# Attention of a two-layer decoder trunk: three low parts move from GpSimd to VectorE, the value products lag the scores by three and five steps, and split and whole blocks alternate

## The chip, the cores and the metric

The kernel runs on one core of one Trainium2 chip. The metric is the time of one execution on the device in microseconds (us); lower is better. The core has five engines that run side by side: TensorE (PE; its weight loads are shown as PEld), VectorE (DVE), ScalarE (ACT), GpSimd (POOL) and SyncE (SP), which here only issues DMAs. Each works through its own instructions strictly in order. An instruction that has to wait for another engine therefore holds up everything behind it on its own engine.

## The reference, cut to what matters

The reference computes two decoder layers over 1024 positions with a model width of 1024. The change is in the first layer's attention: 12 heads, queries and keys of 96 features, values of 64, causal.

```python
def causal_dense_attention(q, k, v):          # q, k: 1024 x 12 x 96, v: 1024 x 12 x 64
    scale = dk ** -0.5
    sc = einsum('bqhd,bkhd->bhqk', q_blk, k) * scale
    sc = where(k_idx <= t_idx, sc, NEG)
    p = softmax(sc, axis=-1)
    return einsum('bhqk,bkhd->bqhd', p, v)

def reference(x, mem, positions, ...):
    for i in range(2):
        hn = rmsnorm(x, attn_norm_g[i])
        mix, q_cross = mla_mixer(...) if i % 2 == 0 else swa_mixer(...)   # MLA calls the attention above
        cross = memory_cross_attention(q_cross, mem_n, w_mem_kv[i])
        x = x + concatenate([mix, cross]) @ w_o[i]
        x = x + squared_relu_mlp(rmsnorm(x, mlp_norm_g[i]), mlp_w_up[i], mlp_w_down[i])
    return rmsnorm(x, final_norm_g)
```

All results must have float32 accuracy.

## The kernel before

**Split products.** The kernel's fast matmul form takes operands rounded to a shorter float (`fp32r` in the rows). To keep float32 accuracy a value is split: the high part is a rounded copy, made by ScalarE, and the low part (the rest) is the value minus the high part, made by a subtraction (`split`, L96 to L103). A product is then three matmuls: high by high, high by low, low by high. Whoever doesn't split uses the full float32 matmul, which counts as two instructions in the rows.

**The stages.** First the projections into queries, keys and values; then the attention of layer 0, the subject here; then the output projection (`pswo`), the MLP, and the same for layer 1. In the trace the attention runs from about 251 us to 516 us.

**The attention.** A head's scores are computed transposed: keys on the partitions, queries along the row. The 1024 queries are two groups G of 512, the 1024 keys are 8 blocks k of 128. Causality leaves 12 blocks (G, k) for each head; blocks on the diagonal are narrower: 512, 384, 256 or 128 queries wide (`width`). The table `blocks` sets their order within a head: (1,0), (0,0), (1,4), (0,1), (1,5), (0,2), (1,6), (0,3), (1,7), (1,1), (1,2), (1,3). I number these places 0 to 11. The last head has an order of its own, `blocks_end`.

For each block:

- `scores`: three matmuls of queries (`qh`, `ql`) and keys (`kh`, `kl`) into a bank of PSUM `pss`, with one more for the causal mask on the diagonal; then ScalarE's exponential into `p` (L855). A block in `WHOLE` is left so. Any other is split into `ph` (ScalarE) and `pl` (VectorE, L100).
- `values`: the product with the values, accumulated over a group's blocks in a PSUM bank `pso`. A whole block is one full float32 matmul with `vf`; a split block is three matmuls, `ph` by `vh`, `ph` by `vl`, `pl` by `vh`. When a group is done ScalarE copies it out (`on`) and DMAs store it. `vh` carries 64 columns of ones, which give the softmax denominators; `rc_split` and `rc_mul` later apply their reciprocals to the stored outputs (`psrc`).

The loop (from L956) walks the blocks of all heads in one sequence. At step n it issues the scores of block n, then some work of later heads, then the values of block n − 2 (`LV = 2`). Where one of the two blocks is 128 wide, their matmuls alternate.

The work of later heads is: `row_max`, a first cheap score product `psx` with VectorE's maximum over it (eight for each head, L729 to L731; those wider than 512 share one buffer of two banks); `max_row`, which transposes the maxima (`psxt`, L711) and writes them as a 97th feature into the queries by DMA; `head_tiles`, which loads the next-but-one head's queries and keys into single buffers `q32`, `k32` and splits them (high parts `qh`, `kh` by ScalarE, low parts `ql`, `kl` by GpSimd, `lo_eng`); and `v_tiles`, which splits the values (`vh` by ScalarE, `vl` by GpSimd, `vf` a copy by VectorE). The reciprocal tiles of `rc_split` use the buffers `q32` and `k32` too.

A scheduler then settles the order on each engine: it may move instructions ahead of where the code issues them when it thinks their inputs are ready.

Of the kernel before, what the change touches and what calls it, by code (L numbers as in the profile page):

```python
# [55 lines left out]
def trunk(  # L56
# [38 lines left out]

    def split(src, hi, lo, scale=None, lo_eng=None):  # L96

        if scale is None:
            nc.scalar.activation(hi, src, AF.Copy)  # L99
            (lo_eng or nc.vector).tensor_tensor(lo, src, f32(hi), ALU.subtract)  # L100
        else:
            nc.scalar.activation(hi, src, AF.Copy, scale=scale)
            nc.vector.scalar_tensor_tensor(lo, src, scale, f32(hi), ALU.mult, ALU.subtract)  # L103
# [588 lines left out]
    def head_tiles(h):  # L692
        r = slice((h % 2) * 64, (h % 2) * 64 + 64)
        q32 = hb.tile([96, S], F32, tag="q32", bufs=1, name=f"q32_{h}")
        k32 = hb.tile([96, S], F32, tag="k32", bufs=1, name=f"k32_{h}")
        nc.sync.dma_start(out=q32[0:64], in_=qn[h // 2][r, :])
        nc.sync.dma_start(out=q32[64:96], in_=qr[h // 4][(h % 4) * 32 : (h % 4) * 32 + 32, :])
        nc.sync.dma_start(out=k32[0:64], in_=kn[h // 2][r, :])
        nc.sync.dma_start(out=k32[64:96], in_=krs)
        qh, ql, kh, kl = bufs_[h % 3]  # L700
        if h in (1, 2):
            head_ones(h)
        split(q32, qh[0:96], ql[0:96], lo_eng=nc.gpsimd)
        split(k32, kh[0:96], kl[0:96], lo_eng=nc.gpsimd)

# [110 lines left out]
    def v_tiles(h):  # L816
        vh, vl, vf = vbufs[h % 2]
        src = v[:, :, h * 64 : (h + 1) * 64]
        if h < 2:
            nc.gpsimd.memset(f32(vh[:, :, 64:128]), 1.0)  # L820
            nc.gpsimd.memset(vf[:, :, 64:128], 1.0)
        nc.scalar.activation(vh[:, :, 0:64], src, AF.Copy)
        nc.gpsimd.tensor_tensor(vl, src, f32(vh[:, :, 0:64]), ALU.subtract)
        nc.vector.tensor_copy(vf[:, :, 0:64], src)

    blocks = [(1, 0), (0, 0), (1, 4), (0, 1), (1, 5), (0, 2), (1, 6), (0, 3), (1, 7), (1, 1), (1, 2), (1, 3)]

    blocks_end = [(1, k) for k in (0, 4, 5, 6, 7, 1, 2, 3)] + [(0, k) for k in range(4)]
    WHOLE = {(1, k) for k in (0, 4, 5, 6, 7)}
    probs, po_ = {}, {}  # L830
# [4 lines left out]
    def scores(h, G, k):  # L835
# [17 lines left out]
        def then():  # L853
            p = at.tile([P, 512], F32, tag="p", bufs=5, name=f"p{h}_{G}_{k}")
            nc.scalar.activation(p[:, c0:], ps, AF.Exp, scale=SC)  # L855
            if (G, k) in WHOLE or (h == H - 1 and G == 0):
# [9 lines left out]
    def values(h, G, k):  # L866

        vh, vl, vf = vbufs[h % 2]
        c0 = 512 - width(G, k)
        order = [b[1] for b in blocks if b[0] == G]  # L870
        first, last = k == order[0], k == order[-1]
        if first:
            po_[G] = ps1(f"pso{h}_{G}")
        po = po_[G]
        pr = probs.pop((h, G, k))
        mms = []
# [3 lines left out]

        if len(pr) == 1:
            mm(po[:, c0:], vf[:, k, :], pr[0][:, c0:], start=first, stop=last)
        else:
            ph, pl = pr
            mm(po[:, c0:], vh[:, k, :], ph[:, c0:], start=first, stop=False)
            mm(po[0:64, c0:], vl[:, k, :], ph[:, c0:], start=False, stop=False)
            mm(po[:, c0:], vh[:, k, :], pl[:, c0:], start=False, stop=last)

# [17 lines left out]
    def last_o(G, tmp):  # L906

        nc.vector.reciprocal(tmp, po_[G][64:128])
        nc.vector.tensor_tensor(qn[5][64:128, G * 512 : (G + 1) * 512], po_[G][0:64], tmp, ALU.mult)

# [44 lines left out]
    muls = iter(())  # L955
    for n in range(len(seq) + LV):  # L956
        ms, mv = [], []
        if n < len(seq):
            ms, then_s = scores(*seq[n])
        if n >= LV:  # L960
            mv, then_v = values(*seq[n - LV])

        mix = []
        if ms and mv and P in (width(*seq[n][1:]), width(*seq[n - LV][1:])):
            while ms and mv:
# [33 lines left out]
        if n == 10 * NB + LV + 1:  # L999
            rc_split(1)  # L1000
        if n == 10 * NB + LV + 8:
            muls = rc_mul(1)
        if n == 11 * NB + LV + 1:
            rc_split(2)
        if n == 11 * NB + LV + 6:
            muls = rc_mul(2)
    for _ in muls:
# [925 lines left out]
```

## Time and profile before

| | |
|---|---|
| median of 3 runs | 2217.64 us (2213.63 to 2220.11) |
| profiled execution | 2218.95 us, span 2216.1 us |
| mean granted TensorE clock | 0.986 |
| PE busy | 2151.1 us, 97% of the span |
| DVE / ACT / POOL busy | 1486.9 / 1018.5 / 235.1 us |

The span runs from the first to the last instruction; 2.85 us lie outside it. TensorE is busy nearly throughout, so the questions are where it is not, and where it is busy at a lower clock: the granted clock is a share of 2.4 GHz, and it is either 1.0 or 0.5 (1.2 GHz) at any moment, so a mean of 0.9 says that a fifth of the stretch ran at half speed. In a row of the timeline the first number is the start in us, the second the time taken; a bracket at the end gives how long the engine had been idle before and what ended that. Matmuls are pipelined: one starts before the one ahead has ended, so their pace is read from the starts.

### The profile page before, as it was taken

What the parts mean: (1) busy time and instruction counts of PE and PEld (TensorE: products, weight loads), DVE (VectorE), ACT (ScalarE), POOL (GpSimd) and SP (SyncE); (2) the same over time, 40 slices, a digit from 0 to 9 for tenths busy, and PEclk for the clock granted to TensorE, in tenths of its full rate; (3) what the DMA queues carried; (4) which work ended last, traced back from release to release, by engine and by line L of the source; (5) the groups of instructions that cost most, each with busy time, mean ns of one, the idle gap of its engine ahead of it and who ended that gap; (6) DMA issues with size and microseconds to landing.
All of it is one profiled execution on the core that took longest, in us unless ns stands there. A gap on an engine that the chain in (4) does not pass through costs nothing.

```text
span 2216.1 us, 28995 instructions
## 1 busy us (share of the span) xinstructions
PE 2151.1 (97%) x10005; PEld 1717.9 (78%) x10005; DVE 1486.9 (67%) x2789; ACT 1018.5 (46%) x2154; POOL 235.1 (11%) x263
## 2 busy tenths in 40 slices
PE   7999989999999999999999899999999999999998
PEld 6888656567878888888888788768788888788886
DVE  7566656566797777695757443675987776785565
ACT  5454455465543333344445363674633333444452
POOL 0023332220000000000001033350000000000000
PEclk9999989899999999999999999999999999999999
DMA  7202121134234444873534111113254445954442
GB/s 245 65 1 72 44 58 42 42 85 150 77 135 151 143 146 153 292 277 104 183 114 124 53 47 40 48 49 116 85 171 157 152 145 168 328 190 142 130 119 86
DMA packets 171232, 272.97 MB, mean 123 GB/s; under 512 B 15713, under 2 KB 71758, under 8 KB 171086
## 3 DMA queue, kind: packets, MB, share of 16 engines
q1 hardware_dynamic: 164228, 253.80, 35.6%
q0 software_dynamic: 4016, 13.12, 1.6%
q10 hardware_dynamic: 2842, 4.22, 0.6%
q8 instruction: 78, 1.28, 0.2%
q14 instruction: 68, 0.56, 0.1%
HBM read 181.69 MB, written 76.81 MB: 117 GB/s over the span
## 4 chain that ended last, share of the span: by engine, by line
PE 88%; DVE 5%; ACT 3%; DMA 1%; issue 1%; POOL 0%; SPq 0%; DVEq 0%; ACTq 0%; POOLq 0%
PE psu L1306 5%; PE psu L1307 5%; PE psu L1305 5%; PE psy L1591 5%; PE psy L1593 5%; PE psy L1592 5%; PE psz L1591 4%; PE psz L1593 4%; PE psz L1592 4%; PE psv L1305 4%; PE psv L1306 4%; PE psv L1307 4%; PE pss L845 4%; PE pso L879 3%; PE pswo L110 3%; PE pswo L108 3%
## 5 line engine op out<-in xcount | busy, mean ns | idle before, releaser
L855 ACT ACTIVATE p<-pss 128x512 f32<-128x512 f32 (+2 forms) x144 | 69.2, 487 | 96.6 <-PE pss L845 91.4
L99 ACT ACTIVATE i<-mr 128x512 fp32r<-128x512 f32 x78 | 49.3, 632 | 121.8 <-PE psu L1306 42.9
L731 DVE TENSOR_REDUCE m<-psx 128x1 f32<-128x640 f32 (+7 forms) x96 | 72.3, 754 | 43.9 <-PE psx L730 42.7
L1591 PE MATMUL psy<-g 128*128 128x512 f32 x256 | 99.9, 390 | 0.0
L1592 PE MATMUL psy<-g 128*128 128x512 f32 x256 | 99.6, 389 | 0.0
L1593 PE MATMUL psy<-g 128*128 128x512 f32 x256 | 99.4, 390 | 0.0
L100 DVE TENSOR_TENSOR pl<-p,ph 128x512 fp32r<-128x512 f32 (+3 forms) x80 | 73.1, 917 | 30.3 <-ACT ph L99 30.2
L99 ACT ACTIVATE g<-i 128x512 fp32r<-128x512 f32 x79 | 49.7, 629 | 93.2 <-PE psz L1592 46.2
L100 DVE TENSOR_TENSOR g<-i,g 128x512 fp32r<-128x512 f32 x79 | 55.3, 700 | 46.0 <-ACT g L99 45.8
L99 ACT ACTIVATE uh<-i 128x512 fp32r<-128x512 f32 x66 | 41.6, 631 | 86.2 <-PE psy L1592 40.7
L100 DVE TENSOR_TENSOR uh<-i,uh 128x512 fp32r<-128x512 f32 x66 | 45.5, 690 | 44.3 <-ACT uh L99 44.2
L1591 PE MATMUL psz<-g 128*128 128x512 f32 x192 | 74.7, 389 | 0.0
L1592 PE MATMUL psz<-g 128*128 128x512 f32 x192 | 74.7, 389 | 0.0
L1593 PE MATMUL psz<-g 128*128 128x512 f32 x192 | 74.7, 389 | 0.0
L100 DVE TENSOR_TENSOR i<-mr,i 128x512 fp32r<-128x512 f32 x78 | 53.7, 688 | 24.2 <-ACT i L99 24.2
L845 PE MATMUL pss<-qh,kh 97*128 97x512 f32 (+2 forms) x144 | 68.4, 478 | 0.6 <-DMA qh<-mhl 0.6
L1694 POOL TENSOR_TENSOR wsr<-wsr,gcol 128x1024 f32<-128x1024 f32 x12 | 24.2, 2017 | 355.3 <-DVE ul L1336 284.1
L1516 DVE TENSOR_TENSOR mqf<-mqq,mqf 128x512 f32<-128x512 f32 x64 | 43.1, 687 | 26.3 <-DMA mqq<-in_mlp_w_down_dram 26.0
L845 PE MATMUL pss<-ql,kh 97*128 97x512 f32 (+2 forms) x144 | 60.5, 420 | 0.0
L99 ACT ACTIVATE i<-d 128x512 fp32r<-128x512 f32 x44 | 27.8, 633 | 70.0 <-PE psu L1306 39.6
L1593 PEld LDWEIGHTS psy<-g 128*128 128x128 f32 x256 | 48.0, 188 | 10.0
L1592 PEld LDWEIGHTS psy<-g 128*128 128x128 f32 x256 | 48.1, 188 | 9.9
(623 smaller groups left out, 7018.8 us busy)
## 6 DMA issues: line engine op xcount, KB each, us to landing
i<-hd SPq DMA_DIRECT2D x154, 256.0 KB
hd<-uh SPq DMA_DIRECT2D x76, 256.0 KB
hd<-ul SPq DMA_DIRECT2D x76, 256.0 KB
mr<-in_mlp_w_up_dram SPq DMA_DIRECT2D x36, 512.0 KB
hd<-x SPq DMA_DIRECT2D x72, 256.0 KB
mr<-hd SPq DMA_DIRECT2D x70, 256.0 KB
d<-in_mlp_w_up_dram SPq DMA_DIRECT2D x32, 512.0 KB
mqq<-in_mlp_w_down_dram SPq DMA_DIRECT2D x32, 512.0 KB
```

The source lines that it names most:

```text
L99: nc.scalar.activation(hi, src, AF.Copy)
L100: (lo_eng or nc.vector).tensor_tensor(lo, src, f32(hi), ALU.subtract)
L108: nc.tensor.matmul(ps, ah, bh, start=first and i == 0, stop=False)
L731: nc.vector.reduce_max(m8s[h][:, i : i + 1], ps[:, :n], axis=AX, negate=True)
L845: return lambda: nc.tensor.matmul(o, a, b, skip_group_check=True, **kw)
L855: nc.scalar.activation(p[:, c0:], ps, AF.Exp, scale=SC)
L1305: nc.tensor.matmul(ps, wh[:, k, :], xh[:, k, :], start=p in (1, 2, 5) and k == 0, stop=False, skip_group_check=True)
L1306: nc.tensor.matmul(ps, wh[:, k, :], xl[:, k, :], start=False, stop=False, skip_group_check=True)
L1307: nc.tensor.matmul(ps, wl[:, k, :], xh[:, k, :], start=False, stop=k == 3, skip_group_check=True)
L1591: nc.tensor.matmul(ps, ah[:, j, :], bh, start=p in (1, 5, 2) and k == 0, stop=False, skip_group_check=True)
L1592: nc.tensor.matmul(ps, ah[:, j, :], bl, start=False, stop=False, skip_group_check=True)
L1593: nc.tensor.matmul(ps, al[:, j, :], bh, start=False, stop=k == NP - 1, skip_group_check=True)
```

## The change

There are three parts.

1. In `split` the choice of engine is dropped: `ql`, `kl` and `vl` are subtracted by VectorE, not GpSimd.
2. The values are issued in two parts. At step n come first the low part of block n − 5 (`LB = 5`: the one matmul with `pl`, only for split blocks), then the rest of block n − 3 (`LV = 3`: the whole block, or the two matmuls with `ph`). The buffers follow: `p` 5 to 4, `pl` 3 to 4. The start of `rc_split` and `rc_mul` is now 6 and 11 steps into the head behind each group of heads.
3. Block (1,2) is whole for each head, so that in `blocks` every second block is split; the last head's order becomes (1,0), (1,1), (1,4), (1,3), (1,5), (1,2), (1,6), (1,7), then the four of G = 0, with (1,1) and (1,3) split. Before it was (1,0), (1,4) to (1,7), then (1,1), (1,2), (1,3) split, then the four of G = 0.

```diff
-    def split(src, hi, lo, scale=None, lo_eng=None):
+    def split(src, hi, lo, scale=None):
         if scale is None:
             nc.scalar.activation(hi, src, AF.Copy)
-            (lo_eng or nc.vector).tensor_tensor(lo, src, f32(hi), ALU.subtract)
+            nc.vector.tensor_tensor(lo, src, f32(hi), ALU.subtract)
...
-        split(q32, qh[0:96], ql[0:96], lo_eng=nc.gpsimd)
-        split(k32, kh[0:96], kl[0:96], lo_eng=nc.gpsimd)
+        split(q32, qh[0:96], ql[0:96])
+        split(k32, kh[0:96], kl[0:96])
...
-        nc.gpsimd.tensor_tensor(vl, src, f32(vh[:, :, 0:64]), ALU.subtract)
+        nc.vector.tensor_tensor(vl, src, f32(vh[:, :, 0:64]), ALU.subtract)
...
-    WHOLE = {(1, k) for k in (0, 4, 5, 6, 7)}
+    def whole(h, G, k):
+        return k not in (1, 3) if G else h == H - 1
...
-            p = at.tile([P, 512], F32, tag="p", bufs=5, name=f"p{h}_{G}_{k}")
+            p = at.tile([P, 512], F32, tag="p", bufs=4, name=f"p{h}_{G}_{k}")
-            pl = at.tile([P, 512], F32R, tag="pl", bufs=3, name=f"pl{h}_{G}_{k}")
+            pl = at.tile([P, 512], F32R, tag="pl", bufs=4, name=f"pl{h}_{G}_{k}")
...
+        if late and whole(h, G, k):
+            return [], lambda: None
+        if late:
+            mm(po[:, c0:], vh[:, k, :], probs.pop((h, G, k, "late"))[:, c0:], start=False, stop=last)
...
-    LV = 2
+    LV, LB = 3, 5
...
+        for lag, late in ((LB, True), (LV, False)):
+            if 0 <= n - lag < len(seq):
+                a, b = values(*seq[n - lag], late)
+                mv += a
+                then.append(b)
...
-        if n == 6 * NB + LV + 3:
-            rc_split(0)
-        if n == 7 * NB + LV:
-            muls = rc_mul(0)
...
+            if n == GRP[c + 1] * NB + LB + 1:
+                rc_split(c)
+            if n == GRP[c + 1] * NB + LB + 6:
+                muls = rc_mul(c)
```

What this makes of TensorE's order is shown at the passage from the fourth head to the fifth (`_1_0` is the fifth head's first block; the names lack the head's number, the last number only counts). Before:

```order
L879 MATMUL pso_1_3131<-pl_1_1_3260,vh_2459 128x512
L845 MATMUL pss_1_0_3296<-qh_2445,kh_2447 128x512
L845 MATMUL pss_1_0_3296<-ql_2446,kh_2447 128x512
L845 MATMUL pss_1_0_3296<-qh_2445,kl_2448 128x512
L729 MATMUL psx_5_3302<-kh_2451,qh_2449 128x512
L729 MATMUL psx_5_3302<-kh_2451,qh_2449 128x256
L730 LDWEIGHTS identb
L730 MATMUL psx_5_3302<-dmask,identb 128x128
L879 MATMUL pso_1_3131<-ph_1_2_3274,vh_2459 128x512
L879 MATMUL pso_1_3131<-ph_1_2_3274,vl_2460 64x512
L879 MATMUL pso_1_3131<-pl_1_2_3275,vh_2459 128x512
```

The low part `pl_1_2` is used right behind its `ph_1_2`, with only one block of scores between two such low parts. In the changed kernel the same place reads:

```order
L852 MATMUL pss_1_0_3266<-ql_2446,kh_2447 128x512
L882 MATMUL pso_1_3130<-ph_1_1_3236,vh_2459 128x512
L852 MATMUL pss_1_0_3266<-qh_2445,kl_2448 128x512
L882 MATMUL pso_1_3130<-ph_1_1_3236,vl_2460 64x512
L729 MATMUL psx_5_3275<-kh_2451,qh_2449 128x512
L729 MATMUL psx_5_3275<-kh_2451,qh_2449 128x256
L730 LDWEIGHTS identb
L730 MATMUL psx_5_3275<-dmask,identb 128x128
L852 MATMUL pss_0_0_3284<-qh_2445,kh_2447 128x512
L882 MATMUL pso_1_3130<-p_1_2_3248,vf_2461 128x512
```

Here `ph_1_1` stands alone; its low part `pl_1_1` comes only after two more blocks of scores, (0,0) and (1,4), and two more `psx`; block (1,2) has become one product of the whole `p`.

VectorE's order at the same place, where `m` is the maximum over a `psx`. Before:

```order
L100 TENSOR_TENSOR pl_1_1_3260<-p_1_1_3257,ph_1_1_3259 128x512
L731 TENSOR_REDUCE m_5_3244<-psx_6_3278 128x1
L100 TENSOR_TENSOR pl_1_2_3275<-p_1_2_3272,ph_1_2_3274 128x512
L731 TENSOR_REDUCE m_5_3244<-psx_5_3302 128x1
L100 TENSOR_TENSOR pl_1_3_3290<-p_1_3_3287,ph_1_3_3289 128x512
L731 TENSOR_REDUCE m_5_3244<-psx_3_3321 128x1
L100 TENSOR_TENSOR pl_0_0_3318<-p_0_0_3315,ph_0_0_3317 128x512
L731 TENSOR_REDUCE m_5_3244<-psx_4_3340 128x1
```

In the changed kernel:

```order
L100 TENSOR_TENSOR pl_1_1_3237<-p_1_1_3234,ph_1_1_3236 128x512
L731 TENSOR_REDUCE m_5_3224<-psx_6_3250 128x1
L100 TENSOR_TENSOR kl_1881<-k_6_3313,kh_1880 96x1024
L731 TENSOR_REDUCE m_5_3224<-psx_5_3275 128x1
L100 TENSOR_TENSOR pl_1_3_3263<-p_1_3_3260,ph_1_3_3262 128x512
L824 COPY vf_2461<-v 128x8x64
L731 TENSOR_REDUCE m_5_3224<-psx_3_3296 128x1
L100 TENSOR_TENSOR ql_1879<-q_6_3312,qh_1878 96x1024
L100 TENSOR_TENSOR pl_0_0_3293<-p_0_0_3290,ph_0_0_3292 128x512
L731 TENSOR_REDUCE m_5_3224<-psx_4_3307 128x1
```

The subtraction `pl_1_2` is gone; `kl` and `ql` of the seventh head have come in, `kl` ahead of the maximum over `psx_5`, `ql` ahead of `pl_0_0`.

## Rows read from the trace of the kernel before

**Rows 1.** Page, part 1: busy us (share of the span) xinstructions of each engine

```profile
PE 2151.1 (97%) x10005; PEld 1717.9 (78%) x10005; DVE 1486.9 (67%) x2789; ACT 1018.5 (46%) x2154; POOL 235.1 (11%) x263
```

**Rows 2.** Busy time by stretch: stretch, length, five engines, clock, DMA; attention and parts

```profile
251.00:516.00 265.00, 244.75 (x1152) 160.78 (x1153) 164.61 (x216) 150.89 (x301) 70.21 (x39) 0.93 0.25 61
251.00:280.00 29.00, 22.76 (x111) 14.56 (x112) 23.96 (x24) 15.65 (x30) 16.19 (x10) 0.97 0.25 55
280.00:425.00 145.00, 134.00 (x638) 88.26 (x637) 87.07 (x115) 79.77 (x162) 36.03 (x20) 0.91 0.18 42
425.00:445.00 20.00, 17.85 (x71) 11.70 (x69) 9.32 (x14) 11.05 (x21) 5.94 (x3) 0.83 0.39 92
445.00:516.00 71.00, 70.13 (x340) 46.26 (x339) 44.26 (x63) 44.42 (x90) 12.06 (x6) 0.98 0.33 95
```

**Rows 3.** Waits from 251 to 516 us: who for whom, total, times, longest

```profile
PE pso L879 <- DVE pl L100: 16.2, 14, 2.0
PE psx L729 <- ACT kh L99: 2.1, 1, 2.1
PE psx L729 <- DVE m L731: 1.0, 2, 0.7
```

**Rows 4.** Timeline, 341 to 348 us: GpSimd, VectorE, TensorE

```profile
341.99 2.38 POOL L100 TENSOR_TENSOR kl<-k,kh 96x1024 fp32r<-96x1024 f32 x1 [10.86 <-ACT kh L99]
...
342.46 2.46 DVE L100 TENSOR_TENSOR pl<-p,ph 128x512 fp32r<-128x512 f32 x1 [0.38 <-ACT ph L99]
344.84 0.94 DVE L731 TENSOR_REDUCE m<-psx 128x1 f32<-128x768 f32 x1
...
344.97 0.50 PE L879 MATMUL pso<-pl,vh 128*128 128x512 f32 x1 [1.62 <-DVE pl L100]
347.91 0.80 PE L879 MATMUL pso<-pl,vh 128*128 128x512 f32 x1 [0.48 <-DVE pl L100]
```

**Rows 5.** Groups by line and shape: count, busy us, mean ns, idle before

```profile
L100 DVE TENSOR_TENSOR pl<-p,ph 128x512 fp32r<-128x512 f32 x47 | 53.6, 1143 | 25.9 <-ACT ph L99 25.7
...
L100 DVE TENSOR_TENSOR i<-mr,i 128x512 fp32r<-128x512 f32 x78 | 53.7, 688 | 24.2 <-ACT i L99 24.2
...
L100 DVE TENSOR_TENSOR wsl<-wsr,wsh 128x1024 fp32r<-128x1024 f32 x6 | 8.6, 1428 | 12.7 <-ACT wsh L99 12.7
L100 DVE TENSOR_TENSOR wf<-wsr,wf 128x1024 fp32r<-128x1024 f32 x6 | 7.3, 1224 | 15.6 <-ACT wf L99 15.6
...
L99 ACT ACTIVATE kh<-k 96x1024 fp32r<-96x1024 f32 x11 | 11.6, 1052 | 0.0
```

**Rows 6.** Timeline of TensorE, one head from `psxt` to `psxt`

```profile
359.39 0.28 PE L711 MATMUL psxt<-ident,m 128*8 128x128 f32 x1
...
368.28 0.50 PE L879 MATMUL pso<-pl,vh 128*128 128x512 f32 x1 [1.57 <-DVE pl L100]
371.24 0.50 PE L879 MATMUL pso<-pl,vh 128*128 128x512 f32 x1 [0.81 <-DVE pl L100]
380.17 0.27 PE L711 MATMUL psxt<-ident,m 128*8 128x128 f32 x1
```

**Rows 7.** Timeline of TensorE: a split block's three products, a whole block's pair

```profile
498.17 0.39 PE L879 MATMUL pso<-ph,vh 128*128 128x512 f32 x1
...
498.96 0.49 PE L938 MATMUL psrc<-rTq,sel 4*128 4x512 f32 x1
...
500.38 1.02 PE L879 MATMUL pso<-p,vf 128*128 128x512 f32 x2
501.33 0.49 PE L938 MATMUL psrc<-rTq,sel 4*128 4x512 f32 x1
```

**Rows 8.** Busy time by stretch, 5 us each, behind and with narrow blocks

```profile
420.00:425.00 5.00, 5.00 (x29) 3.21 (x28) 3.07 (x6) 1.18 (x3) 0.00 (x0) 1.00 0.02 5
425.00:430.00 5.00, 5.00 (x23) 3.62 (x22) 2.14 (x5) 2.27 (x7) 0.00 (x0) 0.85 0.32 75
...
490.00:495.00 5.00, 5.00 (x24) 3.10 (x22) 1.12 (x3) 3.98 (x9) 0.00 (x0) 1.00 0.12 28
```

More of the change, by code (lines that the diff above doesn't have):

```diff
@@ L822, in v_tiles, with blocks_of @@
         nc.scalar.activation(vh[:, :, 0:64], src, AF.Copy)
-        nc.gpsimd.tensor_tensor(vl, src, f32(vh[:, :, 0:64]), ALU.subtract)
+        nc.vector.tensor_tensor(vl, src, f32(vh[:, :, 0:64]), ALU.subtract)
         nc.vector.tensor_copy(vf[:, :, 0:64], src)
     blocks = [(1, 0), (0, 0), (1, 4), (0, 1), (1, 5), (0, 2), (1, 6), (0, 3), (1, 7), (1, 1), (1, 2), (1, 3)]
-    blocks_end = [(1, k) for k in (0, 4, 5, 6, 7, 1, 2, 3)] + [(0, k) for k in range(4)]
-    WHOLE = {(1, k) for k in (0, 4, 5, 6, 7)}
+    blocks_end = [(1, k) for k in (0, 1, 4, 3, 5, 2, 6, 7)] + [(0, k) for k in range(4)]
+    def blocks_of(h):
+        return blocks if h < H - 1 else blocks_end
+    def whole(h, G, k):
+        return k not in (1, 3) if G else h == H - 1
     probs, po_ = {}, {}
@@ L853, in then @@
         def then():
-            p = at.tile([P, 512], F32, tag="p", bufs=5, name=f"p{h}_{G}_{k}")
+            p = at.tile([P, 512], F32, tag="p", bufs=4, name=f"p{h}_{G}_{k}")
             nc.scalar.activation(p[:, c0:], ps, AF.Exp, scale=SC)
-            if (G, k) in WHOLE or (h == H - 1 and G == 0):
+            if whole(h, G, k):
                 probs[(h, G, k)] = (p,)
@@ L864, in scores, with values @@
         return mms, then
-    def values(h, G, k):
+    def values(h, G, k, late):
         vh, vl, vf = vbufs[h % 2]
         c0 = 512 - width(G, k)
-        order = [b[1] for b in blocks if b[0] == G]
+        order = [b[1] for b in blocks_of(h) if b[0] == G]
         first, last = k == order[0], k == order[-1]
[L872 to L875, printed above, removed]
         mms = []
@@ L879, in mm @@
             mms.append(lambda: nc.tensor.matmul(o, a, b, skip_group_check=True, **kw))
-        if len(pr) == 1:
-            mm(po[:, c0:], vf[:, k, :], pr[0][:, c0:], start=first, stop=last)
-        else:
[L884 to L887, printed above, removed]
+        if first and not late:
+            po_[(h, G)] = ps1(f"pso{h}_{G}")
+        po = po_[(h, G)]
+        if late and whole(h, G, k):
+            return [], lambda: None
+        if late:
+            mm(po[:, c0:], vh[:, k, :], probs.pop((h, G, k, "late"))[:, c0:], start=False, stop=last)
+        else:
+            pr = probs.pop((h, G, k))
+            if len(pr) == 1:
+                mm(po[:, c0:], vf[:, k, :], pr[0][:, c0:], start=first, stop=last)
+            else:
+                ph, probs[(h, G, k, "late")] = pr
+                mm(po[:, c0:], vh[:, k, :], ph[:, c0:], start=first, stop=False)
+                mm(po[0:64, c0:], vl[:, k, :], ph[:, c0:], start=False, stop=False)
+                last = False
         def then():
@@ L906, in last_o @@
     def last_o(G, tmp):
-        nc.vector.reciprocal(tmp, po_[G][64:128])
-        nc.vector.tensor_tensor(qn[5][64:128, G * 512 : (G + 1) * 512], po_[G][0:64], tmp, ALU.mult)
+        po = po_[(H - 1, G)]
+        nc.vector.reciprocal(tmp, po[64:128])
+        nc.vector.tensor_tensor(qn[5][64:128, G * 512 : (G + 1) * 512], po[0:64], tmp, ALU.mult)
     GRP = [0, 6, 10, 11]
@@ L946, in trunk @@
     head_tiles(1)
-    LV = 2
+    LV, LB = 3, 5
     NB = len(blocks)
-    seq = [(h,) + b for h in range(H) for b in (blocks if h < H - 1 else blocks_end)]
+    seq = [(h,) + b for h in range(H) for b in blocks_of(h)]
     ahead = {}
@@ L955, in trunk @@
     muls = iter(())
-    for n in range(len(seq) + LV):
-        ms, mv = [], []
+    for n in range(len(seq) + LB):
+        ms, mv, then = [], [], []
         if n < len(seq):
             ms, then_s = scores(*seq[n])
-        if n >= LV:
-            mv, then_v = values(*seq[n - LV])
+        for lag, late in ((LB, True), (LV, False)):
[3 more added lines that the diff above has]
+                then.append(b)
         mix = []
-        if ms and mv and P in (width(*seq[n][1:]), width(*seq[n - LV][1:])):
+        if ms and mv and P in [width(*seq[n - lag][1:]) for lag in (0, LV, LB)]:
             while ms and mv:
@@ L983, in trunk @@
             f()
-        if n >= LV:
-            then_v()
+        for f in then:
+            f()
         next(muls, None)
@@ L994, in trunk @@
             nc.scalar.activation(sel, sel32, AF.Copy)
-        if n == 6 * NB + LV + 3:
-            rc_split(0)
-        if n == 7 * NB + LV:
-            muls = rc_mul(0)
[L999 to L1006, printed above, removed]
+        for c in range(3):
+            if n == GRP[c + 1] * NB + LB + 1:
+                rc_split(c)
+            if n == GRP[c + 1] * NB + LB + 6:
+                muls = rc_mul(c)
     for _ in muls:
```

## The prediction

> **What bounds the kernel now.** I read the page's busy times first: TensorE is busy for 2151.1 of 2216.1 us [rows 1]. What can be gained lies in the remaining 65 us and in stretches at half clock. Next come the busy times by stretch. In the attention, 251 to 516 us, TensorE is busy for 244.75 of 265 us and its mean granted clock is 0.93 [rows 2]. So 20.25 us are idle. The clock has two levels, 1.2 and 2.4 GHz, and a mean of 0.93 means that 14% of the stretch ran at the lower one. What was done there would have taken half as long, so 0.07 × 265 = 18.6 us are lost to it (17.2 to 19.9 by the rounding of 0.93). The two add up to 38.9 us, and nothing else in the stage can be given back. The other engines are far from full there: VectorE 164.61 us, ScalarE 150.89, GpSimd 70.21.
>
> The waits name who ends TensorE's idle time: 16.2 of the 20.25 us end with VectorE's `pl`, in 14 waits; one of 2.1 us ends with ScalarE's `kh`, two of 1.0 us in all with the maxima `m` [rows 3]. The timeline shows why `pl` is late [rows 4]. A subtraction `pl` of 128x512 that begins at 342.46 takes 2.46 us. GpSimd's `kl` runs from 341.99 for 2.38 us, and `pl` ends about half a microsecond behind it; TensorE stood idle for 1.62 us until then. The groups say the same: these 47 `pl` take 1143 ns on average, while VectorE's subtraction of the same shape takes 688 ns elsewhere [rows 5]. So VectorE almost stands still while GpSimd subtracts, and TensorE uses `pl` too early to sit that out.
>
> **The change part by part.** *Engine.* GpSimd's subtractions leave; VectorE gets them. Their shapes on VectorE are not in the trace; the nearest rows are subtractions of 128x1024, 1224 ns, and 1428 ns for those that run beside GpSimd's multiplications [rows 5]. I take 1.22 us, since GpSimd now does next to nothing in this stage; 1.43 is the other end. The values' low part has the shape of the 688 ns row. In the stage 11 heads have their queries and keys split (the count of `kh` in [rows 5]), which adds 22 × 1.22 = 26.8 us to VectorE, and 12 their values, 12 × 0.69 = 8.3. It gives back as much, 8.3, for the `pl_1_2` of 12 heads, and 47 × (1.143 − 0.688) = 21.4 us of slowed `pl`: 164.6 + 26.8 + 8.3 − 8.3 − 21.4 = 170 us of some 238. VectorE stays under three quarters and can't bound the stage by its sum. It can by its order, and that is the wait that the change adds. `kl` waits for ScalarE's `kh`, which waits for the last scores that read the old keys; behind `kl` in VectorE's queue stands the maximum over `psx_5`, and TensorE's `psx_4` needs the buffer that this maximum frees. Between the two, TensorE has two blocks of 512 with the mask, a whole product and `psx_3`. By the pace of rows 7, three products in 0.79 us and a pair in 0.95, that is at least 2 × 0.8 + 0.95 = 2.5 us. VectorE needs 1.22 for `kl` and 0.94 [rows 4] for the maximum, 2.2 us in all. It fits with little to spare, and `kl` can begin earlier than I count, so I cost it at nothing. If the cover is gone it costs up to the whole of `kl`.
>
> *Lag.* `pl` is now used five blocks behind its scores. Three more blocks of 1 to 2 us each lie between, more than the longest `pl` wait of 2.0 us [rows 3], and the cause of the slow `pl` is gone too. So I let the 16.2 us go. `ph` and the whole `p` get one block more, which costs TensorE nothing; it has the same matmuls in another order.
>
> *Whole (1,2).* Three fast matmuls become one full one. From the first of the three to the next product (`psrc`) is 498.96 − 498.17 = 0.79 us, from the pair to the same kind of product 501.33 − 500.38 = 0.95 [rows 7]. That is 0.16 us more for each of 12 heads: 1.9 us lost. Other neighbours could make it 1 to 4. What ScalarE saves, a copy in each head, is off the path.
>
> *Reciprocals and tail.* `rc_mul` now starts three blocks earlier for the first group of heads, so that `q32` and `k32` come free sooner; the `kh` wait of 2.1 us, at 437 us, sits behind these buffers. I expect 0.5 to be left of the idle 2.15 us from 425 to 445 [rows 2]. At the end the last values come one step later behind the scores, with no scores beside them. I cost it at 1 us (0 to 3).
>
> *What stays.* Idle by stretch now and expected [rows 2]: 251 to 280 us, 6.24, of which 2 stay, since the first head has no earlier head to fill in and its two subtractions now stand ahead of the first maxima; 280 to 425, 11.0, of which 0.5 stay; 425 to 445, 0.5; 445 to the end, 0.87, of which 1 is left; the tail 1. That is 5.0 us (1 to 10).
>
> The clock follows idle time loosely. A head at full clock took 20.78 us with 2.38 idle [rows 6], so about 18.4 without. Elsewhere it fell with no idle time in front: from 425 to 430 us the clock is 0.85, though TensorE was busy throughout the five microseconds before; these were the narrow blocks. From 490 to 495 us, again narrow blocks, it stayed at 1.00 [rows 8]. The narrow blocks stay in the change, so I let some of the loss stay: 5 of 18.6 us (0 to 12).
>
> **Sum.** 20.25 − 5.0 idle, 18.6 − 5 of clock, less 1.9: 26.95, say 27 us gained. The profiled execution took 2218.95 us, which gives 2192. It stands 1.3 us above the median of the runs, 2217.64; I don't correct for that.
>
> **Rivals.** *The clock doesn't come back.* Idle time goes, but the narrow blocks and short gaps still bring the clock down once in most heads. For: the 425 us row. Against: 445 to 516 us, with 0.87 us idle and as many narrow blocks, has 0.98 [rows 2]. Then 20.25 − 5.0 − 1.9 = 13.4 us are gained: 2205.6. The Trainium skill has a rule for this ("TensorE: Matmul & The Clock Gate", "A second HAM failure mode: psum-queue depth-cycling"): where matmuls cycle through PSUM banks, small pauses between groups make the clock swing between its levels, and throughput stays degraded. By that rule the change, which leaves fewer banks to the scores because the sums `pso` live longer, would be at 2205.6 or above; the row from 445 to 516 us doesn't bear it out.
>
> *VectorE's queue becomes the bound* (the side of slower). `kl` and `ql` each hold the queue, with the ScalarE copy that they wait for: 1.22 + 1.05 [rows 5], twice in each of 11 heads, 50 us. If nothing covered that and the clock stayed as it is, the time is 2218.95 − 20.25 + 50 + 1.9 = 2250.6. It is slower than before from 18.35 / 11 = 1.7 us of stall in each head on. For: `kl` has an earlier place in the queue than any `pl` had to give. Against: the maxima cost only 1.0 us now [rows 3], though they stand behind `pl` of up to 2.46 us [rows 4], and `pl` no longer waits. With half of that point, 0.8 us a head, the gain is 18.35 − 9 = 9.5 us, 2209.5, and a little beyond that there is no change to be told.
>
> *The stall only moves.* The wait for `pl` was also a cover: without it ScalarE's `ph`, or the exponentials that free the score banks, may be late. Half of idle and clock loss would come back: 19.4 − 1.9 = 17.5 us, 2201.4. ScalarE has 150.9 of 265 us [rows 2], so I count this inside the likeliest case.
>
> **How the numbers follow.** The forecast of 2192 has 0.70, with a range of its own of 2184 to 2203. The clock that stays away has 0.16 (2206). VectorE's queue has 0.10: 0.06 around no change and 0.04 slower. Better than my case has 0.04; the floor is 2218.95 − 38.9 + 1.9 = 2182. With unknown costs at their ends the sum runs from 2182 (1 us idle, no clock loss, 1.0 for the whole blocks) to 2206 (10, 12 and 4). The range for 8 in 10 is 2182 to 2208. A measurement of this kernel can tell 0.3%, 6.6 us, from no change. Faster than that: 0.90; within: 0.06; slower: 0.04.
>
> **What would show it.** In the profile after: no GpSimd subtraction between 251 us and the end of the attention; `pl` of 128x512 at about 0.69 us on average; no wait of TensorE on `pl` above 3 us in all; TensorE's idle time in the stage about 5 us, its clock about 0.98; the stage about 238 us long, nearly all of the difference. VectorE's subtraction of 96x1024 at 1.2 us. If the clock stays at 0.93 with little idle time, the first rival holds; if waits of TensorE on `m` grow beyond 10 us, the second. I am wrong if the stage is shorter by less than 15 us, or if the difference lies outside it.

## The result, and the profile after

| | before | after |
|---|---|---|
| median | 2215.64 us (2213.2 to 2220.11, 4 runs) | 2181.66 us (2178.6 to 2188.19, 4 runs) |
| profiled execution | 2218.95 us, span 2216.1 | 2188.19 us, span 2186.5 |
| mean granted clock of that execution | 0.986 | 0.991 |
| attention, first `pss` to first `pswo` | 251.27 to 515.88: 264.6 us | 253.40 to 488.30: 234.9 us |

The ratio is 0.9848 (0.9818 to 0.9879): faster by 34.0 us, 1.5%. The forecast was 2192.0 with a range from 2182; the median lies 0.34 us below that low end. The direction, the place and the mechanism came out; the gain is 7 us larger than the sum gave. A second series of the same kernel (below) gave 2180.34 us, and its profiled execution of 2180.12 us is used as well: the first profiled execution happens to be the slowest of its four runs. One of the six executions of the lag alone (below) took 4285.32 us, for a reason that nothing here shows, and is left out of its numbers.

Page of the kernel after, part 1 (busy us, share of the span, instructions), the counterpart of [rows 1]:

```profile
PE 2139.8 (98%) x9993; PEld 1714.4 (78%) x9993; DVE 1480.1 (68%) x2813; ACT 1009.6 (46%) x2142; POOL 162.1 (7%) x227
```

Busy time by stretch of the same execution (stretch, length, five engines, clock, DMA), as in [rows 2]:

```profile
253.00:488.50 235.50, 232.36 (x1140) 156.41 (x1141) 157.31 (x237) 144.78 (x293) 2.59 (x6) 0.96 0.27 69
253.00:280.00 27.00, 25.87 (x132) 17.33 (x133) 23.95 (x34) 18.07 (x35) 1.66 (x4) 1.00 0.36 83
280.00:425.00 145.00, 144.53 (x752) 99.66 (x750) 99.70 (x155) 92.54 (x190) 0.93 (x2) 1.00 0.25 57
425.00:445.00 20.00, 18.48 (x92) 13.05 (x91) 15.54 (x23) 14.11 (x27) 0.00 (x0) 0.91 0.48 145
445.00:488.50 43.50, 43.47 (x171) 26.37 (x169) 18.11 (x28) 20.06 (x44) 0.00 (x0) 0.84 0.21 69
465.00:480.00 15.00, 15.00 (x37) 8.38 (x36) 3.73 (x7) 5.20 (x10) 0.00 (x0) 0.56 0.24 81
```

From 280 to 425 us the 11.0 us of idle time are down to 0.47 and the clock went from 0.91 to 1.00. The idle time of the whole stage is 3.1 us in place of 20.25. Apart from 425 to 445 us (0.91), only the last head lost time to the clock: 0.84 from 445 us on, mostly in the last row, and that with TensorE busy throughout. The second profile of this kernel has no such loss in the last head:

```profile
251.00:480.50 229.50, 226.03 (x1140) 153.28 (x1141) 157.22 (x237) 144.84 (x293) 2.74 (x6) 0.99 0.28 71
425.00:445.00 20.00, 18.31 (x89) 12.72 (x89) 14.73 (x23) 12.79 (x26) 0.00 (x0) 0.91 0.44 136
445.00:480.50 35.50, 35.48 (x162) 22.17 (x162) 16.86 (x26) 19.41 (x43) 0.00 (x0) 1.00 0.25 80
...
574.50:589.50 15.00, 14.29 (x67) 10.79 (x65) 14.89 (x29) 10.93 (x22) 0.54 (x1) 1.00 0.21 71
```

There the attention runs from 251.5 to 480.4, 228.9 us, 6 less than in the first profile. (The last row is used further below.)

TensorE's waits after (who for whom, total, times, longest), first profile, against [rows 3]: `pl` is gone from the list, `kh` went from 2.1 to 0.5 us, one wait of 1.5 us for a maximum is new.

```profile
PE psx L729 <- DVE m L731: 1.5, 1, 1.5
PE pso L882 <- ACT ph L99: 0.6, 1, 0.6
PE pss L852 <- DMA qh<-mhl: 0.5, 1, 0.5
PE psx L729 <- ACT kh L99: 0.5, 1, 0.5
```

VectorE's subtractions in the stage by shape (count, busy us, mean ns, idle before), against [rows 5]: `pl` fell from 1143 to 684 ns, and the three that came in took what the forecast gave them (1.22, 1.22, 0.69 us).

```profile
L100 DVE TENSOR_TENSOR pl<-p,ph 128x512 fp32r<-128x512 f32 x35 | 23.9, 684 | 11.9 <-ACT ph L99 11.9
L100 DVE TENSOR_TENSOR kl<-k,kh 96x1024 fp32r<-96x1024 f32 x11 | 13.4, 1218 | 4.6 <-ACT kh L99 4.6
L100 DVE TENSOR_TENSOR ql<-q,qh 96x1024 fp32r<-96x1024 f32 x11 | 13.3, 1212 | 2.3 <-ACT qh L99 2.3
L823 DVE TENSOR_TENSOR vl<-v,vh 128x512 fp32r<-128x512 f32 x12 | 8.2, 681 | 0.0
```

One head, from one `psxt` to the next, is best read over five steady heads at full clock. Timeline of TensorE after, the first and the last of six successive `psxt`:

```profile
284.50 0.27 PE L711 MATMUL psxt<-ident,m 128*8 128x128 f32 x1
...
374.27 0.28 PE L711 MATMUL psxt<-ident,m 128*8 128x128 f32 x1
```

That is 89.77 / 5 = 17.95 us a head with no wait in it; before, a head took 20.78 with 2.38 idle [rows 6]. 20.78 − 2.38 is 18.40, and with the dearer block (1,2) it should have been 18.56. Here lies the surprise that the experiments had to explain: 0.6 us a head more were given back than had been idle.

### The profile page after: what moved, and what is told of

Its sections match the earlier page's. It is cut to its first block, busy times and chain, and to the rows that moved or that the text cites. A ratio compares the mean times of both kernels' runs of the same rounds, so it can differ in the third digit from the quotient of the medians.

```text
span 2186.5 us, 28912 instructions
## 1 busy us (share of the span) xinstructions
PE 2139.8 (98%) x9993; PEld 1714.4 (78%) x9993; DVE 1480.1 (68%) x2813; ACT 1009.6 (46%) x2142; POOL 162.1 (7%) x227
## 3 DMA queue, kind: packets, MB, share of 16 engines
q8 instruction: 78, 1.28, 0.2%
## 4 chain that ended last, share of the span: by engine, by line
PE 87%; DVE 6%; ACT 2%; DMA 2%; issue 1%; POOL 0%; SPq 0%; DVEq 0%; ACTq 0%; POOLq 0%
PE psy L1601 5%; PE psy L1603 5%; PE psy L1602 5%; PE psu L1316 5%; PE psu L1317 5%; PE psu L1315 5%; PE psz L1601 4%; PE psz L1602 4%; PE psz L1603 4%; PE pss L852 4%; PE psv L1317 4%; PE psv L1316 4%; PE psv L1315 4%; PE pso L882 4%; PE pswo L110 2%; PE pswo L108 2%
## 5 line engine op out<-in xcount | busy, mean ns | idle before, releaser
L731 DVE TENSOR_REDUCE m<-psx 128x1 f32<-128x768 f32 (+7 forms) x96 | 71.3, 752 | 24.9 <-PE psx L730 24.4
L882 PE MATMUL pso<-p,vf 128*128 128x512 f32 (+3 forms) x152 | 64.9, 509 | 0.0
L1526 DVE TENSOR_TENSOR mqf<-mqq,mqf 128x512 f32<-128x512 f32 x64 | 43.0, 685 | 20.4 <-DMA mqq<-in_mlp_w_down_dram 20.1
L1603 PEld LDWEIGHTS psy<-g 128*128 128x128 f32 x256 | 48.0, 188 | 10.0
L1601 PEld LDWEIGHTS psy<-g 128*128 128x128 f32 x256 | 48.1, 188 | 9.9
L1602 PEld LDWEIGHTS psy<-g 128*128 128x128 f32 x256 | 48.1, 188 | 9.8
```

The source lines that it names most:

```text
L731: nc.vector.reduce_max(m8s[h][:, i : i + 1], ps[:, :n], axis=AX, negate=True)
L882: mms.append(lambda: nc.tensor.matmul(o, a, b, skip_group_check=True, **kw))
L1601: nc.tensor.matmul(ps, ah[:, j, :], bh, start=p in (1, 5, 2) and k == 0, stop=False, skip_group_check=True)
L1602: nc.tensor.matmul(ps, ah[:, j, :], bl, start=False, stop=False, skip_group_check=True)
L1603: nc.tensor.matmul(ps, al[:, j, :], bh, start=False, stop=k == NP - 1, skip_group_check=True)
```

## The experiments

Each was timed against the kernel before on the same chip. "Head" is the mean of five steady heads, read like the two rows above.

| kernel | median us | ratio (95%) | head us | waits for `pl` in these heads |
|---|---|---|---|---|
| engine alone | 2187.1 | 0.9864 (0.9848 to 0.988) | 17.84 | none |
| lag alone | 2189.97 | 0.9885 (0.9865 to 0.9904) | 17.75 | none |
| whole (1,2) alone | 2212.16 | 0.998 (0.9969 to 0.9992) | 20.35 (of three) | 2.07 us each |
| engine and lag | 2181.61 | 0.9836 (0.9822 to 0.9851) | 17.75 | none |
| the same, beside the change | 2181.11 | 0.983 (0.981 to 0.9849) | 17.75 | none |
| engine and whole (1,2) | 2188.49 | 0.9869 (0.9848 to 0.9889) | 18.01 | none |
| the change again | 2180.34 | 0.9832 (0.9813 to 0.9852) | 17.95 | none |
| the change, `kl` and `ql` twice | 2190.87 | 0.9868 (0.9847 to 0.9889) | 17.91 | none |
| engine alone, old TensorE order | 2192.64 | 0.9886 (0.9868 to 0.9904) | 18.64 | 0.53 us each |
| `pl` one step later (smallest lag) | 2190.01 | 0.9868 (0.9852 to 0.9885) | 17.95 | none |

**Engine alone.** The kernel before with the first part of the change.

```diff
-        split(q32, qh[0:96], ql[0:96], lo_eng=nc.gpsimd)
-        split(k32, kh[0:96], kl[0:96], lo_eng=nc.gpsimd)
+        split(q32, qh[0:96], ql[0:96])
+        split(k32, kh[0:96], kl[0:96])
...
-        nc.gpsimd.tensor_tensor(vl, src, f32(vh[:, :, 0:64]), ALU.subtract)
+        nc.vector.tensor_tensor(vl, src, f32(vh[:, :, 0:64]), ALU.subtract)
```

> Only the engine is changed: ql, kl and vl by VectorE; the values lag by two steps and (1,2) is split as before. My theory: pl waited because it took 1.14 us beside GpSimd and was used too early. With the first cause gone, pl takes 0.69 us, but kl (1.22 us) now stands in VectorE's queue right ahead of pl_1_2, so about 1 us of idle time stays in each head. TensorE idle in the attention 8 to 12 us (before 20.25), gain against before 15 to 24 us. Rival (VectorE's queue becomes the bound): idle time of 20 us or more, waits on pl or m above 15 us, gain below 8 us or none. Rival (the engine alone is everything): gain of 30 us or more, idle below 5 us.

**Lag alone.** The changed kernel with the three low parts back on GpSimd, (1,2) split and the last head's order of before.

```diff
+        split(q32, qh[0:96], ql[0:96], lo_eng=nc.gpsimd)
+        split(k32, kh[0:96], kl[0:96], lo_eng=nc.gpsimd)
...
-        return k not in (1, 3) if G else h == H - 1
+        return k not in (1, 2, 3) if G else h == H - 1
```

> Only the lags are changed (three and five steps, with their buffers and the later start of the reciprocals); GpSimd still subtracts, (1,2) is split, and the last head has its order of before. My theory: pl stays slow (above 1 us on average), but nobody waits for it any more; what is left is the maxima m standing behind slow pl. TensorE idle in the attention 3 to 8 us, gain 20 to 30 us. Rival (the contention itself must go): the maxima and pl still come late, idle above 12 us, gain below 12 us.

**Whole (1,2) alone.**

```diff
-    WHOLE = {(1, k) for k in (0, 4, 5, 6, 7)}
+    WHOLE = {(1, k) for k in (0, 2, 4, 5, 6, 7)}
```

> Only block (1,2) is made whole for each head. My theory: the wait on pl_1_2 goes but pl_1_3 and pl_1_1 remain beside GpSimd; idle 10 to 15 us, less 0.16 us of TensorE time lost in each head; gain 3 to 12 us. If the place of the wait simply moves to the next pl, idle stays at 18 us or more and the gain is below 3 us.

**Engine and lag.** The changed kernel with its third part undone: `whole` as in the lag alone, and the last head's order of before.

> The changed kernel with its third part undone: (1,2) is split again for each head and the last head has its order of before. My theory by the prices of the prediction: three fast products cost 0.16 us less than the whole pair, so this is 1 to 4 us faster than the changed kernel if VectorE and ScalarE carry the extra pl and ph; a head at full clock takes 17.8 us from psxt to psxt against 17.95. Rival (ScalarE or VectorE becomes late with one more split): idle of TensorE in the attention 3 us or more above the changed kernel's 3.1, and it is 3 us or more slower than the changed kernel.

The gains against the kernel before, from each series' own medians, are 31 us (engine), 28 (lag), 6 (whole), and 37 for engine and lag together. They don't add up: engine and lag are two cures for one stall, and either removes nearly all of it. My expectation for the engine alone, 15 to 24 us, was too low; the rival beside it, that the engine alone is everything (30 us or more, idle time below 5), is what came, with 31.1 us gained and 4.9 idle. TensorE's waits for `pl` in the whole stage, engine alone (the same view as above):

```profile
PE psx L729 <- ACT kh L99: 2.1, 1, 2.1
PE psx L729 <- DVE m L731: 1.2, 2, 0.8
PE pso L879 <- DVE pl L100: 1.0, 2, 0.6
PE pso L879 <- ACT ph L99: 0.4, 1, 0.4
```

16.2 us became 1.0. The `kh` wait of 2.1 us is still there; it is there, at 2.15, in all four kernels with the old start of the reciprocals (engine alone, with either addition, and the whole block alone), and at most 0.5 in all those where they start as in the change. So the wait went as the forecast said; but all the kernels with the new start also use `pl` later, and no run tells the two apart. The whole block alone leaves the stall in place, with one wait in place of two in a head:

```profile
PE pso L879 <- DVE pl L100: 16.8, 10, 2.1
```

I had expected 10 to 15 us of idle time in the stage; it is 20.1 (240.83 busy of 260.95 us), hardly less than before. So its 6 us need another account, which comes at the end of this section.

**Was it the engine, or the order?** In the run of the engine alone the scheduler had also moved something: TensorE's products with `pl_1_2` and `pl_1_3` stood behind the next block of scores in five of the steady heads (the expectation says six). So I tied them to their old place.

```diff
+        if pin is not None and n < len(seq) and not mix:
+            with tc.issue_after(pin.ins):
+                ms.pop(0)()
+        pin = None
...
         for f in mv:
-            f()
+            pin = f()
...
+            if seq[n - LV][1:] not in ((1, 2), (1, 3)):
+                pin = None
```

> The engine alone, with one thing held as it was in the kernel before: with VectorE subtracting ql, kl and vl the scheduler had also put TensorE's products with pl_1_2 and pl_1_3 behind the next block of scores in six heads, 1.07 us later; here they are tied to their old place ahead of those scores. Theory A (the subtraction beside GpSimd was the stall): the wait for pl stays short; in the run of the engine alone pl_1_2 ends 0.6 us behind the moment at which the old order asks for it, so about 0.6 us idle in each of these heads and steady heads of 18.4 to 18.7 us against 17.84, at least 20 us gained on the kernel before. Theory B (the later place in TensorE's order was the cure): waits of 1.6 and 0.8 us in each head come back, heads of about 20.8 us, and at most 10 us are gained.

Theory A holds: 18.64 us a head, 26 us gained. Timeline of VectorE and TensorE of this kernel, the first and the last `psxt` of six and one head between them:

```profile
289.21 0.27 PE L711 MATMUL psxt<-ident,m 128*8 128x128 f32 x1
...
351.06 1.21 DVE L100 TENSOR_TENSOR kl<-k,kh 96x1024 fp32r<-96x1024 f32 x1
...
351.70 0.47 PE L879 MATMUL pso<-ph,vh 128*128 128x512 f32 x1
352.01 0.39 PE L879 MATMUL pso<-ph,vl 128*64 128x512 f32 x1
352.20 0.68 DVE L100 TENSOR_TENSOR pl<-p,ph 128x512 fp32r<-128x512 f32 x1
...
352.93 0.50 PE L879 MATMUL pso<-pl,vh 128*128 128x512 f32 x1 [0.53 <-DVE pl L100]
353.27 0.39 PE L845 MATMUL pss<-qh,kh 97*128 97x512 f32 x1
353.50 0.23 PE L845 MATMUL pss<-dmaskT,identb 128*128 128x128 bf16 x1
...
382.43 0.27 PE L711 MATMUL psxt<-ident,m 128*8 128x128 f32 x1
```

Two things are to be seen. `pl` takes 0.68 us now, but it stands behind `kl`, 1.21 us, and is late by that: the wait that I had looked for at the maximum behind `kl` is here at `pl_1_2`. And the wait costs more than its bracket says. Without a wait the next product starts 0.23 to 0.24 us after one of 512 (353.27 to 353.50), although it is shown for 0.39. So from 352.01 the next was due at 352.25 and came at 352.93: 0.68 us late, of which the bracket shows 0.53, because the earlier product is still counted as busy. The one behind the wait then takes 0.34 to the next start (352.93 to 353.27) in place of 0.23, another 0.11. That makes 0.26 us beyond the idle time. The heads say the same: 93.22 / 5 = 18.64 here and 89.20 / 5 = 17.84 in the run of the engine alone, whose two `psxt` follow. That is 0.80 apart with one wait of 0.53, so 0.27 is hidden in each wait. Other pairs of heads in the table give the same: the whole block alone and the engine with the whole block have the same products, and 20.35 − 18.01 = 2.34 with one wait of 2.07 (0.27); before and the engine alone are 20.78 − 17.84 = 2.94 apart, with 2.38 in two waits (0.28 each). Two such waits hide 0.55 us, nearly all of the 0.6 a head.

```profile
286.25 0.27 PE L711 MATMUL psxt<-ident,m 128*8 128x128 f32 x1
...
375.45 0.27 PE L711 MATMUL psxt<-ident,m 128*8 128x128 f32 x1
```

**The smallest lag.** The lag alone, with `LV, LB = 2, 3` in place of 3, 5: only the product with `pl` is one step later. The buffers and the start of the reciprocals are those of the lag alone.

> The smallest lag: GpSimd still subtracts ql, kl and vl, the values lag by two steps as before, and only the product with pl comes one step later (two and three in place of three and five); the reciprocals start as in the changed kernel, counted from this lag, and the last head's order is that of before. Theory A (the stall is pl's lateness of 1.72 us and 0.97 us a head, measured from start to start): one block of scores, 1.07 us, takes the second wait wholly and leaves about 0.5 us idle of the first; steady heads of 18.3 to 18.7 us, 15 to 25 us gained. Theory B (VectorE beside GpSimd sets the pace, wherever TensorE asks): heads stay above 19.5 us and at most 10 us are gained.

It takes the whole stall of the steady heads, more than I expected: 17.95 us a head and no wait at all, though `pl` is as slow as before. First the group of `pl` from 251 to 490 us, then the timeline of GpSimd, VectorE and the products with `pl` in one head:

```profile
L100 DVE TENSOR_TENSOR pl<-p,ph 128x512 fp32r<-128x512 f32 x47 | 52.1, 1111 | 10.4 <-ACT ph L99 10.2
```

```profile
350.52 0.68 DVE L100 TENSOR_TENSOR pl<-p,ph 128x512 fp32r<-128x512 f32 x1
...
351.05 2.41 POOL L100 TENSOR_TENSOR kl<-k,kh 96x1024 fp32r<-96x1024 f32 x1 [11.06 <-ACT kh L99]
...
352.49 1.53 DVE L100 TENSOR_TENSOR pl<-p,ph 128x512 fp32r<-128x512 f32 x1
352.93 0.47 PE L882 MATMUL pso<-pl,vh 128*128 128x512 f32 x1
353.48 2.77 POOL L100 TENSOR_TENSOR ql<-q,qh 96x1024 fp32r<-96x1024 f32 x1
...
354.87 0.48 PE L882 MATMUL pso<-pl,vh 128*128 128x512 f32 x1
```

The first `pl` now begins ahead of `kl` and isn't slowed; the second is (1.53 us), ends at 354.02 and is wanted only at 354.87. So the slow subtraction cost TensorE something only because TensorE asked for its result at once. Speed of `pl` and place of its use are two ends of one slack; one block of scores, 1.07 us, is enough of it. Outside the steady heads this kernel still waits: 6.0 us for `pl` in five waits, in the first heads and around 410 and 435 us, which is why it stays behind the change.

**VectorE's queue.** The forecast counted 2.2 us of VectorE's work against a cover of 2.5 us. I had `kl` and `ql` subtracted twice.

```diff
         split(k32, kh[0:96], kl[0:96])
+        nc.vector.tensor_tensor(kl[0:96], k32, f32(kh[0:96]), ALU.subtract)
+        nc.vector.tensor_tensor(ql[0:96], q32, f32(qh[0:96]), ALU.subtract)
```

> The changed kernel, with the subtractions of kl and ql done twice on VectorE (the second copy writes the same values again): 2.44 us more for VectorE in each of 11 heads, 26.8 us in all, on a total of 182.85 from 251 to 516 us. My theory: VectorE's queue has room, the time is at most 3 us longer than that of the changed kernel (2178 to 2192 us), with no head longer than 18.2 us in the steady part. My cover of 2.5 us for kl and one maximum (2.2 us), if it was worked out rightly, is exceeded by 0.9 us where the second kl stands right behind the first: 10 us in all, about 2192. Rival (VectorE's queue is the bound): the whole 2.44 us shows in each head, 27 us, about 2209.

```profile
250.00:280.00 30.00, 25.28 (x115) 15.89 (x113) 27.51 (x35) 16.83 (x30) 1.92 (x4) 0.90 0.24 59
280.00:425.00 145.00, 143.81 (x745) 99.06 (x745) 113.21 (x168) 89.61 (x185) 0.94 (x2) 1.00 0.25 58
...
445.00:490.00 45.00, 45.00 (x184) 27.96 (x184) 21.90 (x32) 23.92 (x50) 0.00 (x0) 0.89 0.27 83
```

By stretch, VectorE has 13.5 us more from 280 to 425 us than in the change, and the steady heads, each with two more subtractions of 1.22 us, are no longer (17.91 us): there the queue has at least 2.4 us a head to spare. That is shown for the sum; the cover at the one place is not tested by it, since the scheduler put the second `kl` three rows further back. But the rows of the change show it. In a steady head the maximum over `psx_5`, right behind `kl`, ends at 328.73, and `psx_4`, which needs its buffer, starts at 330.20 without a wait:

```profile
327.78 0.95 DVE L731 TENSOR_REDUCE m<-psx 128x1 f32<-128x768 f32 x1
...
330.20 0.46 PE L729 MATMUL psx<-kh,qh 96*128 96x512 f32 x2
```

That leaves 1.5 us, where the forecast had counted 0.3.

The doubled kernel is 10.5 us slower than the change beside it, though, and not the 3 that I allowed. In this profile that is the first head, where TensorE waited 3.2 us for maxima between 272 and 277 us and the clock is 0.90 up to 280 us, and a fall of the clock in the last head like that in the first profile of the change. So the queue has no such room in the first head. The rival's 2209 us is far off.

**What the whole (1,2) is worth.** Engine and whole (1,2), with the values' lag of before: both edits as shown above.

> The kernel before with two parts of the change: ql, kl and vl by VectorE, and block (1,2) whole; the values lag by two steps as before. Theory (a whole (1,2) helps only while pl is late; otherwise it costs about 0.2 us a head): a steady head of 17.84 + 0.2 = 18.0 us and a total about 2.4 us longer than with the engine alone, ratio to the kernel before 0.986 to 0.990. Rival (the whole block saves by itself, as the 6 us of its own run): about 6 us shorter than with the engine alone, ratio 0.983 to 0.985.

18.01 against 17.84 us a head: 0.17 lost. With the lag it is 17.95 against 17.75, 0.20. So engine and lag without it should beat the change by 2.4 us, and I ran it again beside the change:

> The changed kernel with part 3 undone, again, beside the changed kernel on one chip, to see whether it beats it. Theory (the whole (1,2) costs 0.2 us in each of 12 heads): 2.4 us shorter than the changed kernel at the same clock, 0.1 per cent, with the spread of the clock (about 10 us) larger than that; span times clock about 2.4 us lower. Rival (the whole block frees ScalarE of a copy in each head and so pays): not shorter, or longer.

> The changed kernel again, for more of its runs and another profile. Theory (its runs differ by falls of the clock alone): times from 2177 to 2190 us, higher where the clock is lower, while span times mean clock stays from 2166 to 2170 us in each run as in the four so far; a steady head of 17.95 us as in the first profile. Rival (something else varies, such as a DMA that lands late): span times clock varies by as much as the times, over 8 us.

2181.11 against 2180.34 us, with intervals that cover each other: it isn't faster. Its attention is 1.3 us shorter (253.8 to 481.4 against 251.5 to 480.4), and it waits 0.9 us at the first `pswo` products, which the change doesn't. No version tried beats the change by what can be measured.

The eight runs of the change lie between 2178.6 and 2188.19 us. Span times mean clock lies between 2166.7 and 2170.1 in all of them, 3.4 us, of which the rounding of the clock to 0.001 is 2. So what varies from run to run is the time at half clock, and the theory of that expectation holds.

The same product sorts the gains, if it is taken as an estimate of the time at full clock. Its means over the runs are 2189.2 for the kernel before (17 runs), 2168.7 for the engine alone, 2171.6 for the lag alone, 2189.4 for the whole block alone, 2168.2 for engine and lag, 2175.3 for the smallest lag and 2167.9 for the change. So some 21 us of the change's 34 are time at full clock, and the engine alone gives nearly all of these. The rest is time at half clock that did not come. The 6 us of the whole block alone are of this kind only: its clock is 0.990 in the mean, where the kernel before has 0.988. Why it falls less there was not found.

## Why the prediction was right, and where it was not

*Who was late, and the cure.* Right. `pl` was late, and no wait for it is left. [rows 4] read as "VectorE almost stands still while GpSimd subtracts", and the mean of 684 ns without GpSimd bears it out. What I had not seen is that engine and lag are each enough.

*The price of the subtractions.* 1.22 us was right. The other end, 1.43, came from a misread row: of the six `wsl` of [rows 5] only one ran beside a GpSimd multiplication, and it took 2.46 us; the other five took 1.21 to 1.23. VectorE's sum of 170 us came out as 157.3: the narrower `pl`, slowed too before, gave back 5.9 us that I had left out, and the rest was not looked into.

*The floor.* This step failed: "The two add up to 38.9, and nothing else in the stage can be given back", and with it the head of "about 18.4 without" and the low end of 2182. Idle time is what a trace shows between the modelled end of one product and the start of the next, and a waiting pipeline hides 0.27 us of each wait in it. With the 14 waits of [rows 3] that is an estimate of 14 × 0.27 = 3.8 us. The second profile gives the account of the stage, 264.6 − 228.9 = 35.7 us: idle 20.25 − 3.5 = 16.8; clock 18.6 − 1.8 = 16.8 (0.91 in 20 us is left); the whole blocks −2.4. The rest is 4.5 us (3.2 to 5.9 by the rounding of the 0.93 in [rows 2]), and 3.8 of it is this. As a total, 35.7 us stay below the 37.0 that the floor allowed (38.9 − 1.9), because idle time and clock loss did not go to nothing; it failed as an account of what can be given back. The median fell 0.34 us below the low end by this together with the terms of clock and of outside below. The Trainium skill ("Perfetto Trace Analysis", "Identifying the Most-Contended Engine") says that the share of time in which matmuls are busy is no good measure of how close a kernel is to its limit, since they are pipelined, and names the share of weight loads among the better ones. The rows agree on the first point: TensorE's busy time in the stage fell by 18.7 us, from 244.75 [rows 2] to 226.03, and the clock less the whole blocks accounts for only 16.8 − 2.4 = 14.4 of them. The weight loads went from 160.78 of 265 us [rows 2], 61%, to 153.28 of 229.5, 67%; whether a floor read from them would have held, no run shows.

*Idle time left.* 5.0 forecast, 3.1 and 3.5 measured. The first stretch has 1.1 to 1.3 in place of 2; the tail, costed at 1, shows no wait; one wait of 1.5 for a maximum, at 439 us, was not foreseen.

*Clock.* 5 us of loss expected to stay. It was 1.8 in one profile and 8.8 in the other (0.91 in 20 us, 0.84 in 43.5), both inside its bounds of 0 to 12. Six of the eight runs have a mean clock of 0.994 or more, nearer the 0.995 of the profile with 1.8 than the 0.991 of the other, so 5 was rather high. Which of the two a run gets is luck as far as is known.

*Whole (1,2).* 1.9 forecast, 2.4 measured, one fifth of a microsecond a head.

*Outside the stage.* Nothing was forecast there. Between the profiled execution of before and the second one of the change lie 38.8 us, 35.7 of them in the stage. Of the other 3.1, 1.1 lie around the span (2.85 us before, 1.72 after). One place behind the output projection gives more than the 2.0 that remain. By stretch, before:

```profile
610.00:625.00 15.00, 11.59 (x50) 8.94 (x50) 13.11 (x26) 8.98 (x18) 0.54 (x1) 0.89 0.17 54
```

TensorE was idle for 3.4 us there and lost 1.65 to the clock; 35.5 us earlier, in the row from 574.5 us above, it is idle for 0.7 at full clock. That is 4.3 us; some 2.3 were lost again at other places. Before, TensorE waited 3.29 us there for ScalarE; the profiles of the other kernels show the gap at 3.3, 2.2 or 0.6 us, without regard to the length of the attention (0.55 in the whole block alone, 3.29 in the lag alone). What sets it was not looked into. For the medians the same 3 us are in the choice to start from 2218.95, where the four runs of before have 2215.64.

*The rivals.* The clock that stays away did not happen: 1.00 from 280 to 425 us, where before it was 0.91. The rule of the Trainium skill that stood beside that rival ("TensorE: Matmul & The Clock Gate", "A second HAM failure mode: psum-queue depth-cycling") speaks of small pauses between groups of matmuls; with 0.47 us idle in those 145 there were hardly any left, so the row does not test it, and shows only that fewer banks for the scores brought no such pauses. VectorE's queue did not become the bound: its work could be doubled at `kl` and `ql`, 2.4 us a head, at no cost to a steady head; only the first head paid. That `kl` can delay something was right in kind; with TensorE's old order it delays `pl_1_2` and costs 0.8 us a head. The stall that moves to ScalarE shows as 0.6 us of `ph` in all.

The errors of size nearly all went one way. Against the second profile, 2192 − 2180.1 = 11.9 us: 4.5 in the stage beyond idle and clock, 3.2 of clock, 1.5 of idle time and 3.1 outside, less 0.5 for the whole blocks. The terms that had bounds kept to them. The first had none, since I had called it a floor, and the range ended at just that floor.

## What to carry to other kernels

A wait of TensorE costs more than the idle time in front of the late product; measure the pace from start to start, in a place without waits, before you call the rest of the time a floor. When an operand is late, ask first whether TensorE could ask for it one block later: here that alone removed the wait without making anything faster. Cures for one stall don't add up, and a scheduler may apply the second when you ask for the first, so look at the order of the engine that waited before you give the credit to an edit. Where the runs differ in granted clock, compare span times clock too: the 6 us of the whole block were clock alone.

## What the runs showed of the hardware

A VectorE subtraction of two operands in SBUF does not share with a GpSimd one, it waits for it. In [rows 4] GpSimd's ends at 344.37 and VectorE's at 344.92, 0.55 us later; in the smallest lag they end at 353.46 and 354.02, 0.56 later, wherever the VectorE one began. In the profile before, 13 `pl` of 128x512 met a GpSimd subtraction already running, and each ends 0.54 to 0.56 us behind one. The Trainium skill ("SBUF — State Buffer", "SBUF: two separate sides") describes the pair of ports that the two share as an exclusive lock, under which the later one blocks until the other is done; both rows agree, and so does the `pl` of 350.52, which began first and took its usual 0.68 us. It goes the other way as well: the GpSimd `ql` of 353.48, shown while `pl` still ran, took 2.77 us and ended 2.23 behind it. An operation with one operand from PSUM did not wait: in the smallest lag VectorE's `qn` (from `psrc`, 128x512) began at 395.98, 0.32 us into a GpSimd subtraction of 1.28, and took its usual 0.69.

The clock can fall with no idle time in front of it: from 465 to 480 us of the first profile TensorE was busy for 15.00 of 15.00 us at a mean clock of 0.56, and in the second profile of the same kernel the last head ran at 1.00. What brings it down there was not found.
